# Softmax times V on one core: an unrolled program of 96 heads becomes a hardware loop of 24 passes over four heads

## The chip, the cores and the metric

One core of a Trainium2 chip. The metric is device time in microseconds, from the first to the last instruction of the core with the launch around it; the profile's "span" is 1.5 to 2.4 us shorter in the profiled runs.

## The reference

```python
batch, n_heads, seq, head_dim = 8, 12, 1024, 64       # 96 heads, all float32
def reference(scores, v):
    scores_max = np.max(scores, axis=-1, keepdims=True)
    attn = np.exp(scores - scores_max)
    attn = attn / (np.sum(attn, axis=-1, keepdims=True) + 1e-8)
    return np.matmul(attn, v).astype(np.float32)
```

A head reads 4 MiB of scores and 256 KiB of v and writes 256 KiB: 4.72 MB, 453 MB for all 96.

## The kernel before

Per head, 128 partitions hold eight rows each. ScalarE takes exp of two rows per partition at a time (an "activation" of 128 x 2048), TensorE transposes each row in eight blocks, VectorE copies the transposed row out of PSUM, and TensorE multiplies it with v, to which a column of ones is added for the sum. VectorE divides. All loads and stores are issued by one queue (SP), with an order that is fixed by hand. The program is a Python loop, so all 96 heads stand unrolled in it: 24,576 TensorE instructions (a load of weights and a matmul for each of 64 transposed blocks and 64 products a head).

```python
EB, G, LAG, NV, AHEAD = 2, 4, 2, 3, 4
s_pool  = tile_pool(bufs=AHEAD);  p_pool = tile_pool(bufs=6);  pt_pool = tile_pool(bufs=5)
ob_pool = tile_pool(bufs=3);  psT_pool = tile_pool(bufs=5, PSUM);  psO_pool = tile_pool(bufs=3, PSUM)
# ... (pools cut to what changes)
def load(n):
    v_sb = v_pool.tile([P, C, D], FP32);    queue(nc.sync.dma_start(out=v_sb[:], in_=v_bh[n]))
    s_nat = s_pool.tile([P, R, SK], FP32)
    step = EB if n == BH - 1 else R                    # the last head in four quarters
    for r in range(0, R, step):
        queue(nc.sync.dma_start(out=s_nat[:, r:r+step, :], in_=sc_bh[n, :, r:r+step, :]))
# ...
for n in range(BH):                                    # 96 heads, unrolled
    nc.gpsimd.tensor_copy(out=vones[:, :, 0:D], in_=v_sb[:])
    for r in range(R):
        if r % EB == 0:
            nc.scalar.activation(out=p_nat[:], in_=s_nat[:, r:r+EB, :], func=EXP)
        for c in range(C):
            nc.tensor.transpose(out=psT[:, c*P:(c+1)*P], in_=p_row[:, c, :], identity=ident16[:])
        nc.vector.tensor_copy(out=pt[:], in_=psT[:])
        if r == R - 1 and n + AHEAD < BH:
            load(n + AHEAD)
        pending.append((n, r, pt, st))
        if len(pending) > LAG:
            finish(pending.pop(0))                     # eight products; after four rows: divide; after eight: store
```

The softmax here doesn't subtract the row's maximum and nothing guards it: scores larger than these inputs give would overflow.

## Time and profile before

| | before |
|---|---|
| time, median (range) | 1089.8 us (1089.6 to 1090.3) |
| span of the profiled run | 1088.4 us |
| busy: PE, ACT, DVE | 72%, 65%, 58% |
| data queue q1, share of the 16 DMA engines | 98.5% |
| instruction queues q8 and q14 | 96 and 24 packets, 0.6% and 0.0% |
| last scores load, landed on all DMA engines | 1077.1 us |

The lines of the page are in the prediction below. Two sets of numbers are not on a page and were taken from the trace's records: when each of the 16 DMA engines reported a transfer as landed ("landings", 4,656 for 291 transfers), and each packet's start and duration on the DMA queues. "Lag" is, for one transfer, the time of a landing after the first of the 16.

One more view of the kernel before, the DMA issues (size in KB, median us from issue to landing), shows how much is queued ahead of each transfer:

```profile
s_nat<-in_scores_dram SPq DMA_DIRECT2D x95, 4096.0 KB, 32.5
out_dram<-out_sb SPq DMA_DIRECT2D x96, 256.0 KB, 32.4
```

A store of 256 KB takes as long as a load of 4 MB (32.4 and 32.5 us): both stand behind two to three heads of loads, 11 us each. The fastest store, at the end, took 2.0 us.

### The profile page before, as it was taken

The page shows a single profiled execution, that of the slowest core. Times are in us where ns is not written, and L with a number is a line of the kernel's source. Part 1 is how long each engine was busy: PE and PEld are TensorE (multiplying, and loading weights), DVE is VectorE, ACT ScalarE, POOL GpSimd, SP SyncE. Part 2 cuts the span into 40 slices and gives each one's busy share as a digit, 9 for nine tenths or more (in the row PEclk, how much of TensorE's full clock was granted, in tenths as well). Part 3 has the DMA queues.
Part 4 walks back from the last instruction along what each step waited for, and adds up shares of the span by engine and source line. Part 5 has one row for each costly group of instructions (what it writes and reads, how often), then busy time and mean ns, then how long its engine had stood idle before and what let it go on. Part 6 is the DMA issues. An engine that isn't in the chain of part 4 may idle for free.

```text
span 1088.4 us, 27687 instructions
## 1 busy us (share of the span) xinstructions
PE 782.8 (72%) x12288; PEld 743.7 (68%) x12288; DVE 628.2 (58%) x1156; ACT 704.0 (65%) x385; POOL 60.1 (6%) x102
## 2 busy tenths in 40 slices
PE   3767777676777767677776767777676777767676
PEld 3667667676766767677676767677676767767676
DVE  2556556565555655556565655655565565556555
ACT  4667576666757666665766666575665757566675
POOL 0000000000000000000000000000000000000000
PEclk9888878778787877878888887878888787787888
DMA  9999999999999999999999999999999999999994
GB/s 396 423 430 425 423 423 427 427 426 428 427 422 423 424 431 427 422 426 424 431 425 429 425 426 424 425 429 428 424 423 430 424 426 427 428 420 428 426 398 160
DMA packets 42024, 454.77 MB, mean 418 GB/s; under 512 B 4656, under 2 KB 4656, under 8 KB 29232
## 3 DMA queue, kind: packets, MB, share of 16 engines
q1 hardware_dynamic: 41904, 453.00, 98.5%
q8 instruction: 96, 1.57, 0.6%
q14 instruction: 24, 0.20, 0.0%
HBM read 427.82 MB, written 25.17 MB: 416 GB/s over the span
## 4 chain that ended last, share of the span: by engine, by line
DMA 96%; DVE 1%; PE 1%; issue 0%; SPq 0%; ACT 0%; DVEq 0%; ACTq 0%
DMA out_dram<-out_sb 69%; DMA s_nat<-in_scores_dram 18%; DMA v_sb<-in_v_dram 9%; DVE out_sb L89 1%; PE psT L140 1%; PE psO L77 0%; SPq L120 0%; ACT p_nat L136 0%; DVE pt L146 0%; SPq L115 0%; DVE recip L88 0%; DVEq L89 0%; SPq L96 0%; ACTq L136 0%
## 5 line engine op out<-in xcount | busy, mean ns | idle before, releaser
L136 ACT ACTIVATE p_nat<-s_nat 128x2048 f16<-128x2048 f32 x384 | 702.8, 1901 | 375.8 <-DMA s_nat<-in_scores_dram 364.7
L140 PE MATMUL psT<-ident,p_nat 128*128 128x128 f16 x6144 | 621.6, 264 | 274.5 <-ACT p_nat L136 273.5
L140 PEld LDWEIGHTS <-p_nat 128*128 128x128 f16 x6144 | 524.9, 155 | 301.5 <-ACT p_nat L136 295.2
L146 DVE COPY pt<-psT 128x1024 f16<-128x1024 f16 x768 | 529.0, 691 | 307.2 <-PE psT L140 285.4
L77 PE MATMUL psO<-vones,pt 128*128 128x65 f16 x6144 | 343.0, 204 | 27.3 <-DVE pt L146 26.3
L77 PEld LDWEIGHTS <-pt 128*128 128x128 f16 x6144 | 295.4, 107 | 39.2 <-DVE pt L146 38.3
L89 DVE TENSOR_TENSOR out_sb<-psO,recip 128x256 f32<-128x256 f32 x192 | 73.6, 420 | 98.7 <-DMA out_dram<-out_sb 98.6
L130 POOL CAST vones<-v_sb 128x512 f16<-128x512 f32 x96 | 59.4, 619 | 1007.3 <-DMA v_sb<-in_v_dram 995.5
L88 DVE RECIPROCAL recip<-psO 128x4 f32<-128x4 f32 x192 | 34.1, 178 | 49.9 <-PE psO L77 49.9
L136 ACT ACT_TABLE_LOAD x1 | 1.3, 1283 | 0.7 <-PEq L168 0.7
L64 DVE MEMSET vones<- 128x8 f16 x3 | 0.1, 65 | 0.8 <-PEq L168 0.8
L58 DVE CAST ident<-ident 128x128 f16<-128x128 f32 x1 | 0.2, 227 | 0.4 <-POOL ident masks.py:199 0.4
masks.py:199 POOL TENSOR_SCALAR_AFFINE_SELECT ident<-ident 128x128 f32<-128x128 f32 x1 | 0.3, 294 | 0.1
masks.py:197 POOL MEMSET ident<- 128x128 f32 x1 | 0.2, 205 | 0.3 <-POOLq L168 0.3
L168 POOL MEMSET const-float32-0.0<- 128x1 f32 x1 | 0.1, 99 | 0.2 <-issue 0.2
L168 POOL MEMSET const-bfloat16-1.0<- 128x1 bf16 x1 | 0.1, 102 | 0.0
L168 POOL MEMSET const-uint8-127<- 128x1 uint8 x1 | 0.1, 102 | 0.0
L168 POOL MEMSET const-float32-1.0<- 128x1 f32 x1 | 0.1, 99 | 0.0
## 6 DMA issues: line engine op xcount, KB each, us to landing
s_nat<-in_scores_dram SPq DMA_DIRECT2D x95, 4096.0 KB, 32.5
v_sb<-in_v_dram SPq DMA_DIRECT2D x96, 256.0 KB, 23.5
out_dram<-out_sb SPq DMA_DIRECT2D x96, 256.0 KB, 32.4
s_nat<-in_scores_dram SPq DMA_DIRECT2D x4, 1024.0 KB, 23.8
```

Source lines behind the costliest of these rows:

```text
L58: nc.vector.tensor_copy(out=ident16[:], in_=ident32[:])
L64: nc.vector.memset(vo[:, :, D : D + 1], 1.0)
L77: nc.tensor.matmul(out=psO[:, g, :], lhsT=pt[:, c * P : (c + 1) * P], rhs=st["vones"][:, c, :], start=(c == 0), stop=(c == C - 1),)
L88: nc.vector.reciprocal(out=recip[:], in_=psO[:, :, D : D + 1])
L89: nc.vector.tensor_tensor(out=st["out_sb"][:, r - G + 1 : r + 1, :], in0=psO[:, :, 0:D], in1=recip[:].to_broadcast([P, G, D]), op=mybir.Al ...
L130: nc.gpsimd.tensor_copy(out=vones[:, :, 0:D], in_=v_sb[:])
L136: nc.scalar.activation(out=p_nat[:], in_=s_nat[:, r : r + EB, :], func=EXP)
L140: nc.tensor.transpose(out=psT[:, c * P : (c + 1) * P], in_=p_row[:, c, :], identity=ident16[:],)
L146: nc.vector.tensor_copy(out=pt[:], in_=psT[:])
L168: nc = _bacc.Bacc("TRN2", target_bir_lowering=False, num_devices=1)
```

## The change

The intent: a program that is a 24th as long, in which the four heads of a pass use fixed buffers, with no stop between passes (`iteration_sync="reg_based"`), loads for the next pass issued from within the present one, and no order among stores. Two smaller things change with it: the scores of every fourth head are loaded in two halves from the second pass on (before, only the last head was cut, in quarters), and the numbers of buffers.

```diff
-    for n in range(BH):
-        s_nat, v_sb = loaded.pop(n)
+    for k in range(AHEAD):
+        load(k, k)
+    with tc.For_i(0, BH, AHEAD, iteration_sync="reg_based") as n0:
+        queued.clear()
+        heads(n0)          # the same body for k in 0..3, on s_bufs[k], v_bufs[k], vones_bufs[k]
@@
-        step = EB if n == BH - 1 else R
+    def load_next(k, n0):
+        n = (n0 + (AHEAD + k)) % BH
+        load(k, n, R if k < AHEAD - 1 else R // 2, cond=n0 < BH - AHEAD)
@@
+            for other in stores:          # tc.declare_no_dep(..., across_iterations=True), both ways
+                apart(dma, other)
+                apart(other, dma)
+            apart(dma, dma)
@@  buffers, before -> after (the rest cut)
-    p 6, pt 5, out_sb 3, psT 5, psO 3, vones 3
+    p 8, pt 4, out_sb 4, psT 4, psO 4, vones 4
@@  at the end of each pass
+        while pending:
+            finish(pending.pop(0))
```

## The prediction

1058.2 us for the last landing and 10.8 us of tail give 1069.0 us of span, and with the 1.5 us between span and time 1070.5, given as 1071. Rival A: no run showed yet whether a loop's body would be fetched again, and its 20%, like the 70% for a body that stays, is the author's estimate. The 64 bytes of an instruction are 1.57 MB over 24,576, and a "block", here and in the expectations, is what one packet of q8 carries: 16,384 bytes in the records, so 256 instructions. That a load counts when its slowest DMA engine has delivered can be seen near the end: a load of scores landed on the first engine at 1045.6 us and on the last at 1065.9, and ScalarE's exp of it started at 1066.0.

> **What bounds the kernel now.** I read the page's head and its 40 slices first, then the queues, then the waits of the DMA-issuing queue, and last the tail in narrow windows together with the landing times of single transfers.
>
> ```profile
> span 1088.4 us, 27687 instructions
> PE 782.8 (72%) x12288; PEld 743.7 (68%) x12288; DVE 628.2 (58%) x1156; ACT 704.0 (65%) x385; POOL 60.1 (6%) x102
> ...
> DMA  9999999999999999999999999999999999999994
> GB/s 396 423 430 425 423 423 427 427 426 428 427 422 423 424 431 427 422 426 424 431 425 429 425 426 424 425 429 428 424 423 430 424 426 427 428 420 428 426 398 160
> ...
> q1 hardware_dynamic: 41904, 453.00, 98.5%
> q8 instruction: 96, 1.57, 0.6%
> q14 instruction: 24, 0.20, 0.0%
> ```
>
> No engine is over 72% and DMA is at nine tenths until the last slice, so the DMA engines set the time. Two small rows matter: q8 and q14 carry instructions, not data. q8's 96 packets of 16 KB are 1.57 MB, which is 24,576 TensorE instructions (12,288 loads of weights and as many matmuls) of 64 bytes: the unrolled program of TensorE streams in beside the data. One packet comes every 11 us, one per head.
>
> ```profile
> SPq L115 <- DMA s_nat<-in_scores_dram: 803.6, 89, 10.4
> ```
>
> In the issuing queue's waits, the v load of a head waits until the scores load eight DMAs back has landed. With three DMAs a head (v, scores, store) about two and a half heads stay queued, some 25 us of work. Queues are deep.
>
> ```profile
> 1040.00:1050.00 10.00, 7.21 (x114) 6.77 (x112) 5.85 (x12) 6.58 (x4) 0.62 (x1) 0.83 1.01 422
> 1050.00:1060.00 10.00, 6.98 (x118) 6.62 (x116) 5.93 (x12) 6.29 (x5) 0.62 (x1) 0.83 0.91 366
> 1060.00:1070.00 10.00, 6.29 (x108) 5.87 (x106) 5.26 (x12) 5.76 (x4) 0.62 (x1) 0.80 0.68 268
> 1070.00:1080.00 10.00, 10.00 (x183) 10.00 (x182) 7.92 (x14) 10.00 (x6) 0.00 (x0) 0.86 0.38 154
> ```
>
> The last two columns are the DMA share and GB/s. From 1050 on the share falls to 0.91, 0.68, 0.38 while loads are still on their way: some DMA engines are out of work and others are not. The landing times in the trace (16 per transfer, one for each DMA engine) say how this came about. The first scores load lands on all 16 within 0.5 us (13.0 to 13.5). After that the lag of the slowest behind the fastest grows in a straight line: 2.7 us at 110, 8.8 at 462, 13.5 at 726, 18.2 at 991, 20.3 at 1046. Just before the end eight engines lag by 17 to 20 us, the other eight by 0 to 11. The slowest lag goes up in steps of 1.54 us every 88.5 us, which is eight heads. The durations of q8's packets repeat with period eight too (1095, 1084, 1014, 1016, 1073, 1076 ns and so on). I read this as: q8's packets go round eight of the 16 DMA engines, each of those gets 96 / 8 = 12, and each costs that engine 1.54 us of data time (its own 1.07 us and some loss around it). 12 x 1.54 = 18.5 us. A load counts as landed only when the slowest engine has delivered, so the kernel pays all of it. This is far more than the 0.6% mean share suggests: 0.6% of 1088 is 6.5 us spread over 16.
>
> [...]
>
> **The change part by part.** *Loop.* A pass has four heads of 64 transposes and 64 products, each with a weight load: 4 x 128 x 2 = 1024 TensorE instructions, 64 KB[...]. If the body stays resident, q8 falls from 96 packets to those of the first pass or two, under 10, at most one or two per DMA engine. The steady rate then is the fastest engine's of today: its landings at 109.9 and 990.6 are 80 heads apart, 11.01 us a head; the slowest's, 112.6 and 1008.8, 11.20. Difference 0.19 x 96 = 18.6 us, the same as 12 x 1.54.
>
> Where would the last load land? The fastest engine had the last head's first two quarters at 1049.5 and 1051.9; then its queue was dry, as the third quarter was issued only at 1054.4. At 2.4 us a quarter it would have ended at 1056.7. I add 1.5 us for one remaining fetch: 1058.2, against 1079.1 for the slowest today.
>
> *Halves.* The last head ends with a half, not a quarter, so more compute follows the last landing. Two activations of 1.9 us follow: the first rows reach TensorE at +2.0, the last two at +3.9, their transposes (0.53 us a row) and the lagging products (0.3 to 0.45 us a row) end near +5.5; copy 0.7, last products 0.5, reciprocal and multiply 0.6, store 2.3 to land, 1.1 of closing waits: about +10.8. Today it is 1088.4 - 1079.1 = 9.3. The half costs some 1.5 us. In the other passes the halves only add 24 DMAs, whose cost is lost in the queue.
>
> *End of a pass.* The pending products are finished before the next pass, and each engine takes a back-edge. TensorE has 11.2 - 8.15 = 3.0 us to spare per head (782.8 / 96 = 8.15), 12 us per pass[...]. Issuing is late only if it slips by over 17 us, the least that is queued when a split head uses up one of eight places.
>
> *Stores.* In a loop, addresses are registers, and each store would wait for the earlier one; taking the order away only avoids a new wait. Four output buffers for three should end most of the vector engine's waits for stores (98.6 us in 91), which are off the path.
>
> Sum: 1058.2 + 10.8 = 1069.0 us of span; times are 1.5 us above span (1089.93 against 1088.4), so 1070.5, rounded up to **1071 us**, -1.7%.
>
> **The rivals.** *A, the body is fetched again in each pass.* [...] If the packets keep going round eight engines, four blocks a pass change nothing, and five or six mean 15 to 18 per engine, 3 to 6 x 1.54 = +5 to +9 us: 1095 to 1100 with the longer tail. If a block always goes to the same DMA engine, those get 24 each and +18.5 us: about 1109. [...] *B, passes leave holes in the DMA queue*, because the issuing queue stalls at the back-edge, or because the conditional loads with addresses in registers wait for more than the unrolled ones. A hole of 2 us a pass would be +48 us, about 1120 with the gain taken off. Against it: the 17 to 25 us queued, and no barrier between passes. *C, the load rate and not the lag is the limit:* if all 16 engines together cannot keep 11.01 us a head (4.72 MB, 429 GB/s), the gain shrinks. Against it: with a lag of only 2.7 to 4.2 us, between 110 and 198 us, the fastest already ran eight heads in 88.1 us, as later. It would give 1075 to 1085.
>
> **Range and chances.** Resident body 70%: 1066 to 1075. Fetched again 20%: 1092 to 1110. Holes 10%. The range is 1065 to 1098. The bound for faster by over 2% is 1068.1 us, 3 us below my number, and the error of the tail and of the remaining fetches is about that: 0.24. Slower by over 2% (above 1111.7) needs B or the worst of A: 0.07. Within 2%: 0.69.
>
> **What would show it.** Right: q8 falls from 96 packets to about ten; the 16 landings of a load stay within some 3 us to the end; the DMA share stays near 1.0 to the last 15 us and then drops at once; the final load lands near 1058. Wrong in the mechanism: q8 stays at 96 or grows (A), or the DMA share dips once every 44 us (B), or q8 is gone and the lag too but a head still takes 11.2 us (C). The prediction fails upwards if the loop adds waits that the issuing queue cannot hide, downwards if the tail is shorter than 10.8 us.

## The result, and the profile after

The changed kernel took **1072.1 us** (1071.9 to 1072.5, four fast runs) against 1089.8: ratio 0.9838, 95% interval 0.9821 to 0.9855. The prediction was 1071 us, within 2%, in a range of 1065 to 1098.

The head and the slices of the changed kernel's page, then its queues:

```profile
span 1070.1 us, 31933 instructions
PE 752.8 (70%) x12288; PEld 711.3 (66%) x12288; DVE 610.7 (57%) x1157; ACT 733.8 (69%) x408; POOL 60.1 (6%) x102
...
DMA  9999999999999999999999999999999999999995
GB/s 401 430 410 430 430 431 425 432 436 431 431 426 425 434 427 425 431 431 430 433 427 434 420 442 430 421 433 426 429 426 434 432 431 431 429 424 440 430 420 228
...
q1 hardware_dynamic: 44784, 453.00, 99.7%
q8 instruction: 3, 0.05, 0.0%
```

The data is the same (453.00 MB), more instructions are executed, but q8 fell from 96 packets to 3 and q14's row is gone. TensorE executes 25,862 instructions in the 24 passes (1,024 a pass and some 54 for the loop), and q8's packets start at 26.4, 37.9 and 48.2 us and no more within the span: the body is not fetched again in each pass.

The landings of one transfer at four times, in us after the first of the 16 (from the trace's records, sorted):

```
before   110: 0.0 0.1 0.1 0.2 0.3 0.3 0.7 1.1  1.6  1.6  1.7  1.7  2.3  2.4  2.4  2.7
before   462: 0.0 0.0 0.1 0.4 0.8 1.4 3.7 5.0  7.7  7.8  7.9  7.9  8.5  8.5  8.6  8.8
before  1046: 0.0 0.0 0.1 0.4 1.5 4.1 6.8 11.4 17.2 17.4 17.4 18.9 19.9 19.9 19.9 20.3
after    110: 0.0 0.0 0.1 0.1 0.1 0.1 0.1 0.1  0.2  0.2  0.3  0.3  0.4  2.7  2.7  2.9
after   1044: 0.0 0.0 0.1 0.1 0.1 0.1 0.2 0.2  0.3  0.3  0.3  0.4  1.7  2.7  2.7  2.9
```

Before, eight DMA engines fall behind steadily. After, three fall behind once, in the first 70 us, which are as many as q8 has packets, and stay where they are; a fourth drifts to 1.7 us over the whole run, which was not looked into. The records do not name the DMA engine of a landing or of a packet: that it is always the same eight is inferred from the gap between the eighth value and the ninth, and that q8's packets go round these from the steps of 1.54 us in the slowest lag, one in eight heads (88.5 us). The other eight spread too before the change, by up to 11.4 us, and hardly after it; q14's 24 packets are gone as well, but no run separates them.

The windows of the changed kernel at its end (busy times, then the granted clock, the DMA share and GB/s in the last three columns):

```profile
1030.00:1040.00 10.00, 7.83 (x133) 7.71 (x131) 6.30 (x12) 7.61 (x5) 0.62 (x1) 0.84 1.00 426
1040.00:1050.00 10.00, 7.18 (x117) 6.94 (x115) 5.66 (x10) 6.39 (x5) 0.62 (x1) 0.84 0.96 405
1050.00:1060.00 10.00, 9.26 (x167) 8.89 (x166) 7.68 (x16) 9.94 (x7) 0.00 (x0) 0.89 0.66 274
1060.00:1070.00 10.00, 4.58 (x89) 3.96 (x85) 4.79 (x10) 1.05 (x1) 0.00 (x0) 0.96 0.14 52
```

Before, the share fell over some 30 us (0.91, 0.68, 0.38); now it stays near 1.0 until the loads end at 1057 and then drops.

What is left to pay in the end can be put in one table. "Fast" and "slow" are the landings of the last piece of scores on the first and on the last of the 16 DMA engines; the tail is the span minus "slow". In the unrolled kernel its last two quarters were issued late, when the fast engines' queues were dry already, so "fast" is no measure there (they were issued from 1054.4 us on, and the second quarter had landed on the first engine at 1051.9); its slow engines landed the four quarters 2.4 to 2.5 us apart and did not run dry.

| kernel | fast | slow | tail | span |
|---|---|---|---|---|
| before | 1061.4 | 1077.1 | 11.3 | 1088.4 |
| after | 1054.4 | 1057.2 | 12.9 | 1070.1 |

The last load lands 19.9 us sooner, the tail is 1.6 us longer: 18.3 us of span.

The issuing queue of the changed kernel shows a wait that the unrolled one did not have (us in total, times, longest):

```profile
SPq L140 <- DMA out_dram<-out_sb: 236.5, 23, 10.3
```

Twenty-three times, once per back-edge, the first v load of a pass waits until a store has landed. In the trace's records the loop's DMAs land on eight semaphores, 47, 46, 47, 46, 47, 24, 23 and 23 times. This is what 13 DMAs a pass (four v, five scores, four stores) give if the eight are taken in turn from the start of each pass, five of them twice; the first DMA of a pass then takes the semaphore of the one five back, which is the store that the queue is seen to wait for. At that moment one head, some 11 us, is still queued, so nothing runs dry. This becomes important below.

### The profile page after: what moved, and what is told of

Read it like the earlier page. It is cut to its first block, busy times and chain, and to the rows that moved or that the text cites. A ratio compares the mean times of both kernels' runs of the same rounds, so it can differ in the third digit from the quotient of the medians.

```text
span 1070.1 us, 31933 instructions
## 1 busy us (share of the span) xinstructions
PE 752.8 (70%) x12288; PEld 711.3 (66%) x12288; DVE 610.7 (57%) x1157; ACT 733.8 (69%) x408; POOL 60.1 (6%) x102
## 3 DMA queue, kind: packets, MB, share of 16 engines
q1 hardware_dynamic: 44784, 453.00, 99.7%
HBM read 445.64 MB, written 25.17 MB: 440 GB/s over the span
## 4 chain that ended last, share of the span: by engine, by line
DMA 67%; PEld 9%; PE 9%; DVE 5%; ACT 5%; SPq 2%; issue 2%; ACTq 0%
DMA s_nat<-in_scores_dram 67%; PEld L169 7%; PE psT L169 6%; DVE pt L175 5%; ACT p_nat L163 5%; PE psO L105 3%; PEld L105 3%; SPq L140 1%; SPq L143 1%; SPq L124 0%; DVE recip L116 0%; ACTq L163 0%; DVE out_sb L117 0%
## 5 line engine op out<-in xcount | busy, mean ns | idle before, releaser
L175 DVE COPY pt<-psT 128x1024 f16<-128x1024 f16 x768 | 516.3, 690 | 432.3 <-PE L169 214.5
L169 PE MATMUL psT<-ident,p_nat 128*128 128x128 f16 x6144 | 569.7, 251 | 267.3 <-ACT p_nat L163 266.6
L169 PEld LDWEIGHTS <-p_nat 128*128 128x128 f16 x6144 | 492.9, 153 | 282.2 <-ACT p_nat L163 277.7
L105 PE MATMUL psO<-vones,pt 128*128 128x65 f16 x6144 | 374.8, 205 | 45.3 <-DVE pt L175 38.9
L105 PEld LDWEIGHTS <-pt 128*128 128x128 f16 x6144 | 305.2, 106 | 71.8 <-DVE pt L175 70.1
L163 ACT ACT_TABLE_LOAD x24 | 30.8, 1283 | 168.1 <-DMA s_nat<-in_scores_dram 163.2
L117 DVE TENSOR_TENSOR out_sb<-psO,recip 128x256 f32<-128x256 f32 x192 | 81.1, 422 | 4.9
## 6 DMA issues: line engine op xcount, KB each, us to landing
out_dram<-out_sb SPq DMA_DIRECT2D x96, 256.0 KB, 21.1
```

The costliest lines, as they stand in the source:

```text
L105: nc.tensor.matmul(out=psO[:, g, :], lhsT=pt[:, c * P : (c + 1) * P], rhs=st["vones"][:, c, :], start=(c == 0), stop=(c == C - 1),)
L117: nc.vector.tensor_tensor(out=st["out_sb"][:, r - G + 1 : r + 1, :], in0=psO[:, :, 0:D], in1=recip[:].to_broadcast([P, G, D]), op=mybir.Al ...
L163: nc.scalar.activation(out=p_nat[:], in_=s_bufs[k][:, r : r + EB, :], func=EXP)
L169: nc.tensor.transpose(out=psT[:, c * P : (c + 1) * P], in_=p_row[:, c, :], identity=ident16[:],)
```

## The experiments

Theory F: what was gained is the fetching of TensorE's instructions, which had delayed eight of the 16 DMA engines. Rivals: R, the halves and the buffer counts; L, other properties of the loop (unordered stores, different waits of the issuing queue); and that the mean DMA load is what counts, for which 0.6% of fetching is nothing.

### The rest of the change without a loop (e1_unrolled_rest)

```diff
-    NV = 3                                        +    NV = 4
-    ppool 6, ptpool 5, obpool 3, psTp 5, psOp 3   +    8, 4, 4, 4, 4
-        step = EB if n == BH - 1 else R
+        step = R // 2 if n % 4 == 3 else R
```

> The unrolled program with the rest of the change that has a meaning without a loop: every fourth head in two halves (so the last one too), and the buffer counts of the changed kernel (p 8, pt 4, out 4, psT 4, psO 4, vones 4). Theory F (the gain is the fetching of TensorE's instructions that went away): q8 stays at 96 packets, the landings of a load spread to some 20 us at the end, and the time is 1088 to 1093 us (up to 2 us for a half in place of a quarter at the end). Rival R (halves, buffers): 1072 to 1076 us.

Measured: 1085.0 us, ratio 0.9956 (0.9939 to 0.9973). Its queues:

```profile
q1 hardware_dynamic: 44928, 453.00, 98.8%
q8 instruction: 96, 1.57, 0.5%
```

q8 has its 96 packets and the lag at the end is 17.9 us, as expected of theory F, and the time is far above rival R's. But it is also 4.9 us faster than before, where F expected nothing or a small loss, so that R isn't all wrong: a quarter of the gain comes without a loop. The records show packets that took less: q8's 932 ns in the mean (1057 before), the 32 KB data packets 1213 ns in the median (1216). Last scores: fast 1054.5, slow 1072.4, tail 10.5. A head takes the fast engines 10.98 us here (between heads 8 and 88, from the landings of v), as in the changed kernel, against 11.01 before, and what a q8 packet adds to the slow ones is 1.41 us in place of 1.54: over 96 heads and 12 packets these two make up some 4 of the 4.7 us by which the slow landing came earlier. Why the packets are shorter is open: all kernels here with the old buffer counts have the longer ones, all with the new counts the shorter, also the one without halves (told of below). That points to where the buffers lie, but no run changed that alone.

### Longer passes (e2_pass16, e2_pass8)

```diff
-        for k in range(AHEAD):                    # four heads a pass
+        for h in range(HP):                       # HP = 16, or 8
+            k = h % AHEAD
@@  loads: the last four heads of a pass load for the next pass under the condition, the others unconditionally
-    with tc.For_i(0, BH, AHEAD, iteration_sync="reg_based") as n0:
+    with tc.For_i(0, BH, HP, iteration_sync="reg_based") as n0:
```

> The changed kernel with 16 heads per pass, 6 passes: the same loop, register waits, dynamic addresses and unordered stores, but over 4,096 TensorE instructions a pass, 17 blocks of 16 KB. Theory F: [...] q8 is back at about 100 packets, landings spread over some 20 us at the end, 1088 to 1094 us. Rival L (the loop's other properties make it fast: unordered stores, other waits of the issuing queue): 1070 to 1075 us.

> The changed kernel with 8 heads per pass, 12 passes: some 2,150 TensorE instructions, 8.4 blocks of 16 KB[...]. Theory F[...]: about 12 x 9 = 108 packets on q8 and about 1090 us. [...] under rival L: q8 as in the changed kernel (under 10) and 1070 to 1075 us.

Measured: 1100.4 us (ratio 1.0094, 1.0077 to 1.0111) and 1135.0 us (1.0417, 1.0395 to 1.0440). The queue of instructions and the GB/s of the slices, first for 16 heads, then for eight:

```profile
GB/s 396 420 424 429 430 424 429 420 417 426 425 431 425 428 398 411 436 420 435 421 424 395 416 434 421 426 429 387 418 417 427 428 434 419 381 414 430 431 420 171
...
q8 instruction: 107, 1.75, 0.6%
```

```profile
GB/s 398 422 421 429 365 421 423 421 366 423 421 347 412 435 361 410 431 414 383 424 421 367 415 432 368 417 431 374 421 421 424 387 419 418 370 415 428 370 424 218
...
q8 instruction: 107, 1.75, 0.6%
```

The fetching is back in both: 17 or nine packets per pass, at 256 instructions each, give 6 x 17 = 102 and 12 x 9 = 108, and 107 are seen both times (why five more than 102 was not looked into). So a body of eight heads (some 2,150 instructions, 8.4 packets) was fetched about whole in each pass, while one of four heads (3 packets in 24 passes) was not; why, no run shows. Both times, however, miss what F expected (1088 to 1094, about 1090), and the lag is only 6 and 3 us. The slices show dips, one at each back-edge (eleven with eight heads; with 16 heads five back-edges, of which the last four dip clearly). The issuing queue's waits say what they are. The lines are those of the kernel with eight heads, then of that with 16:

```profile
SPq L141 <- DMA s_nat<-in_scores_dram: 476.0, 46, 22.4
```

```profile
SPq L141 <- DMA v_sb<-in_v_dram: 59.1, 5, 12.1
```

With eight heads a pass has 26 DMAs, and with eight semaphores 26 mod 8 is 2: the first load of a pass waits for the DMA two back, a half of the last load, for up to 22.4 us, and the queue runs dry (the DMA share of 130 to 140 us is 0.69). With 16 heads it is 52 mod 8 = 4, and the wait, once in each of five back-edges, is for the v of the last head. I had made a hole that has nothing to do with fetching; that the slow DMA engines catch up in it, which would hide the lag, is my reading of the 6 and 3 us. The runs show that the instructions of a longer body are fetched again; they do not show what that costs.

### Twelve heads per pass (e9_pass12)

As before with HP = 12. With eight semaphores, 39 mod 8 is 7, so the first load of a pass waits for the DMA seven back.

> The changed kernel with 12 heads per pass, 8 passes, 3,220 TensorE instructions a pass, 12.6 blocks. Unlike 8 and 16 heads, its 39 DMAs per pass leave the first load of a pass waiting for a DMA seven back in the queue (4 DMAs a head and 8 semaphores taken in turn from the start of each pass: one back-edge of 8 heads waited only two back, of 16 heads four back), so the queue should not run dry at the back-edge. Theory F: q8 at about 8 x 13 = 104 packets, landings 14 to 20 us apart at the end, 1085 to 1092 us without dips. Rival L (the loop as such): q8 may be 104 as well, but 1070 to 1075 us.

Measured: 1094.0 us, ratio 1.0038 (1.0023 to 1.0054).

```profile
GB/s 395 421 423 431 420 438 421 426 434 423 428 430 422 433 428 423 433 423 429 432 419 426 417 429 424 413 408 434 422 427 420 416 430 424 432 403 409 433 423 133
...
q1 hardware_dynamic: 44784, 453.00, 98.4%
q8 instruction: 104, 1.70, 0.6%
```

q8 has 104 packets, as worked out. The same loop with the same unordered stores and the same halves loses the whole gain and 4 us more, 2 us beyond my range: rival L falls. The slow DMA engines get the last scores at 1077.0 us, the same as in the kernel before (1077.1), against 1057.2 with four heads. The lag was expected to be 14 to 20 us and is 11.4. In the records it stops growing once it reaches about one head (10.98 us). My reading: the second load of a pass still waits seven back, one head is queued at that time, and a DMA engine that is a head ahead runs dry and waits; the issuing queue's waits at the v loads are 10.3 us at the longest (22.4 with eight heads). The time isn't set by the lag itself, 11.4 us here and 15.7 before at the last scores, but by when the slowest engines are done, 1077.0 and 1077.1. That their landing equals the one before is in part chance: with the buffer counts of this kernel the unrolled program had them at 1072.4, and one packet more for each, 104 / 8 = 13 in place of 12, explains about 1.4 of the 4.6 us between. The other 3 us arise in the second half of the run, in which the GB/s of some slices fall to 403 to 416; they are not explained. The tail, 15.2 us, is 2.3 us longer than with four heads. Of these, 1.2 us lie after the last store has landed (3.0 us to the end against 1.8); why was not looked into.

### More to fetch, unrolled (e7_nops, e10_more_pe)

```diff
+            for _ in range(16):
+                nc.tensor.nop(nofuse=True)
```

> The kernel before with 128 no-operations more per head on TensorE: 36,864 instructions, 144 blocks in place of 96, no more work for any DMA of data. Theory F: q8 at about 144 packets, 18 per fetching DMA engine in place of 12, 6 x 1.54 = 9.2 us more: 1097 to 1101 us. Rival (instruction fetching is beside the data and costs nothing; TensorE has 3.0 us per head to spare for 128 no-operations): 1089 to 1092 us.

Measured: 1089.8 us, ratio 0.9999 (0.9983 to 1.0016). The page's head is the same as before (27,687 instructions), and so is q8 (96): the no-operations did not reach the program. The run says nothing of the theory. It was tried again with instructions that do something:

```diff
-            st["psO"] = psO_pool.tile([P, G, M], FP32, tag="psO", name="psO")
+            st["psO"] = psO_pool.tile([P, G, M + 1], FP32, tag="psO", name="psO")
@@ after a row's eight products
+        for i in range(4):
+            nc.tensor.matmul(out=psO[0:1, g, M : M + 1], lhsT=ident16[:, i : i + 1],
+                             rhs=ident16[:, 0:1], start=True, stop=True)
```

> The kernel before with 4 one-column products more per row (64 TensorE instructions more per head, each of hardly any work, into an unused column of PSUM): 30,722 instructions, 120 blocks in place of 96. It does what the no-operations were to do, which never reached the chip (q8 stayed at 96). Theory F: q8 at 120, three packets more on each of eight DMA engines, 3 x 1.4 to 1.54 = 4.2 to 4.6 us more: 1093 to 1096 us, and the lag at the end some 24 us. Rival (fetching lies beside the data): 1089 to 1091 us.

Measured: 1098.0 us, ratio 1.0077 (1.0061 to 1.0092).

```profile
q1 hardware_dynamic: 41904, 453.00, 98.1%
q8 instruction: 120, 1.97, 0.7%
```

q8 has the expected 120 packets for the same data, and the time goes up as F says and the rival doesn't, but by 8.2 us and not by 4.2 to 4.6. The slow DMA engines get the last scores at 1082.2 us, 5.1 later than before, which is 1.7 us for each of three more packets. The other 2.6 us are tail (13.9 against 11.3): TensorE has a quarter more instructions, and in the tail no load hides them. I had left that out. The lag at the end was about 21 us, not 24: as I read it, here too the fast DMA engines ran out of queue.

### The cost put back by itself (e3_one_engine, e3_all_engines)

```diff
+    scratch = sb_pool.tile([1, 4093], FP32, name="scratch")           # or [P, 32]
@@ in the first head of each pass, after its loads are issued
+                    if k == 0:
+                        queue(nc.sync.dma_start(out=scratch[:], in_=v.rearrange("b h s d -> (b h) (s d)")[0:1, 0:4093]))
+                                                                      # or in_=v_bh[0, :, 0, 0:32]
```

> The disputed cost put back by itself: the changed kernel with one further DMA per pass that reads 4,093 numbers (16 KB[...]). 24 packets, 0.39 MB, 0.09% of the bytes, always on the same DMA engine. Theory F (a 16 KB packet on one DMA engine delays that engine's data by 1 to 1.5 us, and the slowest engine sets the end): that engine lags by 24 to 37 us, cut where the queue runs dry, and the time is 1092 to 1108 us. Rival (mean DMA load sets the time): 1073 us.

> Control for the run before: as many further DMAs, one per pass, and as many bytes (16 KB), but as 128 rows of 128 bytes, which go to all 16 DMA engines. Theory F and its rival alike: within 2 us of the changed kernel, 1072 to 1075 us.

Measured: 1093.0 us on one engine (ratio 1.0033, 1.0016 to 1.0050) and 1074.4 us on all (0.9853, 0.9837 to 0.9869). The pages' queue rows, first one engine, then all:

```profile
q1 hardware_dynamic: 44832, 453.40, 98.9%
q8 instruction: 3, 0.05, 0.0%
```

```profile
q1 hardware_dynamic: 48240, 453.40, 99.7%
q8 instruction: 3, 0.05, 0.0%
```

The further DMA of the first run adds 48 packets to q1's 44,784, two for each of 24: one of data and one of the 4-byte packets that the records show with every landing. In the second it adds 3,456, 144 for each: 128 rows and 16 landings, one for each DMA engine. That the one data packet falls on the same engine every time is inferred: the last scores land 18.0 us later than in the second run (below), more than the 24 x 0.61 = 14.6 us that the packets' own records last.

Twenty-four packets of 16 KB, 0.09% of the bytes, make the changed kernel 20.9 us slower when one DMA engine carries them all and 2.3 us slower when 16 share them (and then they are 128-byte rows). The difference is 18.6 us. In the profiled runs it is 18.0, all of it in the landing of the last scores (1076.9 and 1058.9 us; both tails are 13.3). That is 18.6 / 24 = 0.78 us for a packet whose own record lasts 0.61 us, less than the 1 to 1.5 us expected for one, though the time lies in the range. Mean load cannot tell the two apart; the slowest engine can. Here too the lag stayed at about 9.5 us, under the one head (10.98 us) that is queued at the back-edge.

### Stores in order (e4_ordered)

```diff
-            for other in stores:
-                apart(dma, other)
-                apart(other, dma)
-            apart(dma, dma)
```

> The changed kernel with the stores ordered again (each store waits for the one before it to land, also across passes). A store lands some 21 us after issue because it lies behind loads in the same queue, while a head takes 11 us; the issuing queue then holds loads back behind a waiting store. Theory F says that it has nothing to do with fetching: q8 stays under 10, the lag near 3 us, but the queue is thinner; I expect 1075 to 1130 us with dips of the DMA share. If the queue adapts (fewer loads ahead of a store, so stores land sooner), 1072 to 1075.

Measured: 1072.0 us, ratio 0.9834 (0.9818 to 0.9850), the same as the changed kernel: the larger loss that I gave first did not come, and its alternative did. The waits of the issuing queue and the issue row of the stores, for this run:

```profile
SPq L124 <- DMA out_dram<-out_sb: 782.1, 94, 25.4
```

```profile
out_dram<-out_sb SPq DMA_DIRECT2D x96, 256.0 KB, 10.9
```

The same row of the changed kernel:

```profile
out_dram<-out_sb SPq DMA_DIRECT2D x96, 256.0 KB, 21.1
```

The queue does wait for each store (94 waits, 782 us), but a store now lands in 10.9 us after issue in place of 21.1, since loads that would have been ahead of it are held back behind it; about a head (10.98 us) remains queued, and that is enough: the time is the same. The last of the three parts of the change, taking the order of stores away, is worth nothing here.

### A loop that stops between passes (e8_barrier)

```diff
-    with tc.For_i(0, BH, AHEAD, iteration_sync="reg_based") as n0:
+    with tc.For_i(0, BH, AHEAD, iteration_sync="barrier") as n0:
```

> The changed kernel with a loop that stops all engines between passes[...]. All loads for the next pass must then land and be idle at the back-edge: a hole in the DMA of at least the compute of a head (10 us) and some us of start, 23 times: 1250 to 1600 us, with q8 still under 10. It shows that residence alone isn't enough (rival B of the prediction).

Measured: 1366.8 us (one untimed run, state unknown).

```profile
DMA  9969797696886977879779696797967979769680
...
q1 hardware_dynamic: 44784, 453.00, 80.0%
q8 instruction: 4, 0.07, 0.0%
```

The issuing queue's wait at the loop's own line (us in total, times, longest):

```profile
SPq L187 <- DMA s_nat<-in_scores_dram: 461.3, 46, 16.5
```

The body is not fetched again in each pass here either (4 packets on q8), and the time is 294.7 us longer, 12.8 us for each of 23 back-edges, because every load is waited for there (46 waits, two at each). The stops cost far more than the 15.2 us by which the last load came sooner in the loop without them.

### How the last head is cut (e5_whole, e6_half_quarters)

```diff
-        load(k, n, R if k < AHEAD - 1 else R // 2, cond=n0 < BH - AHEAD)
+        load(k, n, R, cond=n0 < BH - AHEAD)                           # e5
+        load(k, n, (R, R, R // 2, EB)[k], cond=n0 < BH - AHEAD)       # e6
```

> The changed kernel without halves: every load of scores whole, the last one too. The last load lands at the same time (1057), but the first half's two activations then start 5 us later; the activations of the last head end at 1057.2 + 7.3 = 1064.5 in place of 1061.0: 3 to 4 us more, 1075 to 1077 us.

> Meant to beat both: the changed kernel with every third head of a pass in two halves and every fourth in four quarters. In the changed kernel's tail ScalarE runs without a break from the landing of the last head but one (1046.3) to 1061.0. With halves there it starts 5 us earlier, and after the last quarter (1057.2) only one activation of 1.9 us is left: ScalarE ends at 1059.1, TensorE and the rest some 2 to 3 us earlier than now: 1069 to 1070.5 us. If the shorter DMAs thin the queue (16 DMAs a pass, eight in flight): 1073 to 1080.

Measured in five rounds: 1074.2 us whole (ratio 0.9857, 0.9842 to 0.9872), 1071.4 us with halves and quarters (0.9832, 0.9819 to 0.9846). The intervals of the latter and of the changed kernel (0.9821 to 0.9855) lie over each other, so it is not shown to beat it. Both times miss what was expected (1075 to 1077, and 1069 to 1070.5) by about 1 us. The landings say where the gain went:

| scores loads per pass | slow | tail | span |
|---|---|---|---|
| 4 (whole) | 1056.0 | 16.2 | 1072.2 |
| 5 (the change) | 1057.2 | 12.9 | 1070.1 |
| 8 (halves and quarters) | 1059.9 | 9.4 | 1069.3 |

Finer loads shorten the tail, 3.3 and 3.5 us, as meant, but each further DMA also costs the DMA engines time: the last scores land 1.2 us later with 23 more and 2.7 us later with the next 69 (counted by their landings: 288, 311 and 380 DMAs), that is 0.04 to 0.05 us each. In 96 heads this gives most of the gain back, to shorten a tail that comes once.

## Why the prediction was right

**The bound.** Right: eight lagging DMA engines, by inference those with the instruction packets, set the end. Their loads end at 1077 in the unrolled kernel and in a loop that fetches (twelve heads), at 1072 in the unrolled kernel with the rest of the change (and so with the buffer counts of both loops), and at 1057 only where q8 is nearly silent (3 packets).

**Rival A, that the body is fetched again, was given 20%.** It did not happen with four heads (3 packets on q8). With eight, 12 and 16 it does (107, 104 and 107), so a short pass was needed and not just convenient; lengths between four and eight heads were not tried.

**Where the last load lands.** Predicted 1058.2, measured 1057.2. The sum was right, its terms less so, and that they met is luck. The fast engines ended at 1054.4 us, 2.3 earlier than the 1056.7 that I worked out (in the unrolled kernel with the rest of the change at 1054.5, so this came without the loop), and the slow ones lag by 2.8 us in place of 1.5: the two errors nearly cancel. I gave all of the gain to the fetching (18.6 us). Of the 19.9 us, 4.7 come without a loop (1077.1 to 1072.4 in the unrolled kernel with the rest of the change), and 15.2 with it. The lag is that of three engines with one packet each. In the landings of both kernels about half of such a first lag arises with the packet (1.3 us) and the rest in the 30 us after it; why is not known.

**The tail.** Predicted 10.8 us, measured 12.9. The unrolled kernel with the same halves and buffer counts (e1_unrolled_rest) comes close to my sum, so that what I had left out comes with the loop. The terms, in us after the last scores have landed, from the traces' records:

| | predicted | e1_unrolled_rest | changed kernel |
|---|---|---|---|
| ScalarE's last exp ends | 3.9 | 3.8 | 3.8 |
| TensorE's last transposes end | 5.5 | 5.6 | 6.5 |
| last store landed | 9.7 | 9.6 | 11.1 |
| end of the span | 10.8 | 10.5 | 12.9 |

The chain of the changed kernel's last work shows TensorE waiting for VectorE's copies between its rows (start, duration, what). Why its rows are slower in the loop is not shown.

```profile
1057.83 0.70 DVE pt L175
1058.53 0.05 issue
1058.57 0.43 PE psO L105 x8
1059.00 0.81 PE psT L169 x13
1059.81 0.70 DVE pt L175
```

The closing waits took 1.8 us, not 1.1. The tail is 2.1 us longer than predicted and the last landing 1.0 us earlier; together they leave the 1.1 us by which the span, 1070.1 us, is over the predicted 1069.0. One reading of the kernel before was wrong and does not enter this sum: I took 1079.1 us for the last landing of scores, which was that of a store. The scores landed at 1077.1, so that tail is 11.3 and not 9.3. That the half in place of a quarter was to cost 1.5 us, and that the tail is 1.6 us longer, agrees by luck: the unrolled kernel with halves has the shorter tail (10.5).

**The halves.** Said to be lost in the queue, except for the end. Against whole loads they cost 1.2 us in the landing of the last scores, so they are not quite lost there, and save 3.3 us of tail.

**The pass's end** was right: no dip in four-head passes, and 11 us queued. The estimate of what is queued at least, 17 us, was too high, because I did not see that the eight semaphores are taken in turn from the start of each pass. Had the number of DMAs per pass been one like 26 or 52, rival B would have come true, as the kernels with eight and 16 heads per pass show.

**The stores.** I wrote that the order, kept, would bring a new wait. It does, and it costs nothing.

**Rival C** (all 16 engines cannot keep the rate) did not come up: a head takes the changed kernel 10.98 us on the fast and on the slow DMA engines alike, and I had said 11.01.

## What to carry to other kernels

In a kernel bound by DMA, look at the slowest of the 16 DMA engines, not at the mean: here 0.09% more bytes on one engine cost 18.6 us more than on all. Spread the landings of one transfer over time, and if they drift apart (here the slowest lag was 0.6 us at 13 us and 20.3 us at 1046), look for traffic that may fall on some engines only, here the 96 instruction packets of a long unrolled program. A loop took that traffic away with about 1,080 TensorE instructions a pass (3 packets) and not with 2,150 (107 packets), and only a loop without a stop was faster (with a stop it took 294.7 us more). Then count the DMAs per pass: with the eight semaphores seen here, taken in turn, their number modulo eight decided how much was queued at the back-edge (with 13 DMAs the queue waited there for the fifth back and no slice shows a dip, with 26 for the second back, up to 22.4 us, and the GB/s fell to 347 to 387 in eleven slices). Finer loads for a short tail cost in every pass (0.04 to 0.05 us a DMA) what they save once.

## What else the records showed

- The activation table is loaded again in each pass: 24 loads of 1,283 ns in place of one.
- A load whose condition is false stays in the counts: 100 v loads are listed, and 445.64 MB of HBM reads where q1 moved the same 453.00 MB in and out as before. 17.8 MB, the four heads that the last pass would have loaded, were not moved, and 311 of the 320 DMAs listed have landings.
